# A hybrid decoder block: the recurrence's sigmoids written as tanh, side tasks cut into more steps, and a smaller permitted lag of side work

## The chip, the cores and the metric

One core of a Trainium2 chip runs the whole program. The metric is device time in microseconds (us), the median of several runs. Five engines work from queues of their own, each in the order in which the program gave it: PE (matrix products; PEld is its weight load), DVE (vector operations), ACT (functions by table, copies), POOL, and SP, which here only issues DMA transfers. An engine whose next instruction waits holds up everything queued behind it.

## What is computed

One decoder layer on x of 256 rows by 2048 columns, all in float32. RMS norm, then one input projection of 2048 to 15,904 columns, three token mixers (a gated linear recurrence; sparse attention over compressed, selected and window keys with 8 heads; forgetting attention with 8 heads), each multiplied by a SiLU gate, projected, scaled by a sigmoid merge gate and summed; an output projection; a gated per-layer embedding. The part that the change rewrites is the recurrence:

```python
rec = jax.nn.sigmoid(einsum(ub, wa) + ba)
inp = jax.nn.sigmoid(einsum(ub, wx) + bx)
log_a = -LRU_C * rec * jax.nn.softplus(-lam)     # LRU_C = 8
a = jnp.exp(log_a)
drive = jnp.sqrt(-jnp.expm1(2.0 * log_a)) * (inp * uc)
_, hseq = lax.associative_scan(linear_combine, (a, drive), axis=1)
```

## The kernel before

**The stream of weights.** All weights pass once through the core in 384 slices, most of 128 x 1024 numbers. I number them from 0 in the program's order; the code calls them `halves`. SP fetches a slice into one of five `raw` buffers. The slice is then cut into two parts, since products run in a rounded 32-bit type and the kernel wants more digits: ACT copies it to the rounded `wh`, then DVE forms the rest, `wl` = raw - wh (`cut`, `split`). PE multiplies wh by the high part of the left operand, wl by the high part, wh by its low part: 12 matmuls of 512 columns for a common slice. A slice of the compression (`cmp`; slices 38, 71 and 91 are such) takes only 8 matmuls of 256 columns, and costs ACT and DVE the same cut.

**The look-ahead.** wh and wl have four buffers (AHEAD + 1). The cut of slice i + 3 is written ahead of the matmuls of slice i, so cut i + 3 can begin when PE has done slice i - 1, and work that stands on ACT's queue behind cut i + 3 was placed there while slice i was being written.

**The side work.** Everything else is a set of generators: `lru_task` (recurrence, four of them, each for two column tiles), `nsa_task` (sparse attention, one for two heads and half of the rows), `fox_task`, `kk_task` and `norm_rows` (keys and queries normed and turned by DVE transposes and DMA, `cross`), `y_split` (gating and splitting a mixer's output for its projection), and so on. Twice per slice `Side.tick` runs a step of each active or urgent task, up to its next `yield`; what the step issues lands on the engines' queues between two cuts. `tick` stops when a clock kept while the program is written says that ACT or DVE would be more than LIMITS ns behind PE: one number for urgent tasks, one for the others, and another pair from the time the first queries (`q0`) are normed. `settle`, `powers` and `landed` let a task pause until that clock thinks that its engines or its DMA are through. So any edit of a task or limit re-deals the side work between the cuts. `need` would force tasks on if a slice's inputs weren't ready.

**The recurrence.** `lru_task` issues four gate functions for each of two column tiles (both results kept, from two PSUM banks, all eight in one step, then both banks given back), then per tile a Tanh of rec and an Exp of rec, a Square, a Sqrt, and DVE products and scans. ACT holds one table of functions at a time; a function of another table is preceded by an ACT_TABLE_LOAD. In a `soft` step of `nsa_task` DVE takes masked minima and ACT's three Exps follow in the same step.

**Names in profile rows.** All instructions have line L206, since one wrapper issues them; they are told by tile: `k_lru` (the recurrence's rec, inp, th), `k_uc`, `k_zt` (a chunk being turned), `k_th`/`k_gl`/`k_gn` (SiLU gates), `kk` (keys' split), `k_pz`/`sp_pc` (softmax), `k_mg` (merge gates), `k_yh`/`k_yl` (a mixer's output, split), `k_hnh`/`k_hnl` (normed input, split).

Of the kernel before, what the change touches and what calls it, by code (L numbers as in the profile page):

```python
# [12 lines left out]
AF = mybir.ActivationFunctionType  # L13
OP = mybir.AluOpType
# [28 lines left out]
VEC = {}  # L43
# [6 lines left out]
N_VEC = _at  # L50
# [273 lines left out]
def block_kernel(ctx: ExitStack, tc: tile.TileContext, io):  # L324
    nc = tc.nc
    clock = Clock()
    V, A, T, G, Q = (Metered(e, clock, n) for e, n in ((nc.vector, "v"), (nc.scalar, "a"), (nc.tensor, "pe"),
                                                      (nc.gpsimd, "g"), (nc.sync, "d")))
# [38 lines left out]
    side = Side(range(4), MOST, clock, ROOMS)  # L367
# [140 lines left out]
    def vcol(name, i=0):  # L508
        return vec[:, VEC[name] + i:VEC[name] + i + 1]
# [78 lines left out]
            split(hi[:, k, :], lo[:, k, :], x_tile(2 * i + k), x0[:, S + 2 * i + k:S + 2 * i + k + 1])  # L588

    def vec_task():  # L590
        a = VEC["lru_gate"]
        V.tensor_scalar(vec[:, a:], vec[:, a:], 0.5, None, op0=OP.mult)
        nl = sml([P, 8], name="nl")
        V.tensor_scalar(nl, vec[:, VEC["lam"]:VEC["lam"] + 8], -1.0, None, op0=OP.mult)
        yield from softplus(spc, nl, 8)
        V.tensor_scalar(spn, spc, -8.0, None, op0=OP.mult)
        V.tensor_scalar(spc, spc, 8.0, None, op0=OP.mult)

        V.scalar_tensor_tensor(gqn, vcol("nq"), SCALE, vcol("nk"), op0=OP.mult, op1=OP.mult)
        V.scalar_tensor_tensor(gqf, vcol("fq"), SCALE, vcol("fk"), op0=OP.mult, op1=OP.mult)  # L600
        yield True
# [58 lines left out]
    def cells(x):  # L660

        return x.rearrange("p (k i b) -> p b k i", b=4, i=32)
# [62 lines left out]
    def lru_task(i):  # L725
# [38 lines left out]
        for c in range(2):  # L764
            ct = 2 * i + c
            for s in range(2):
                g = banks[bs[c]][:, s * S:(s + 1) * S]
                A.activation(rec[own[s], c, :], g[own[s]], AF.Sigmoid, bias=vcol("ba", ct)[own[s]])
                A.activation(inp[own[s], c, :], g[other[s]], AF.Sigmoid, bias=vcol("bx", ct)[other[s]])
        side.back(*bs)  # L770
        yield True
        for c in range(2):
            ct = 2 * i + c
            A.activation(th[:, c, :], rec[:, c, :], AF.Tanh, scale=spc[:, ct:ct + 1])
        for c in range(2):
            ct = 2 * i + c
            A.activation(rec[:, c, :], rec[:, c, :], AF.Exp, scale=spn[:, ct:ct + 1])
        V.tensor_tensor(inp, inp, uc, op=OP.mult)
        yield True

        A.activation(uc, rec, AF.Square)
        V.scalar_tensor_tensor(th, uc, 1.0, th, op0=OP.add, op1=OP.mult)
        yield True
        A.activation(th, th, AF.Sqrt)
        V.tensor_tensor(th, th, inp, op=OP.mult)
        yield True
        for c in range(2):
# [109 lines left out]
    def nsa_task(g, pr, t):  # L897
# [19 lines left out]
        def soft(a, sc):  # L917

            for i, (o, x, msk) in enumerate(zip((pc[:, a, :], ps[:, a, 0, :], ps[:, a, 1, :]), sc,
                                                (cmask[:, t, :], mask[:, P * (2 - n):2 * P], mask[:, P:P + n * P]))):  # L920
                V.tensor_tensor_reduce(o, x, msk, -1.0, FLOOR, OP.add, OP.min, m[:, a, i:i + 1])
            for i, (o, x) in enumerate(((pc[:, a, :], pc[:, a, :]), (cell[:, a, 0], cells(ps[:, a, 0, :])),
                                        (cell[:, a, 1], cells(ps[:, a, 1, :])))):
                A.activation(o, x, AF.Exp, bias=m[:, a, i:i + 1], scale=-1.0, accum_out=s[:, a, i:i + 1])

        if t == 0:
            bs = yield from side.take(2)
            for a in range(2):
                mm3(banks[bs[a]][:, :272], qh[:, a, :], ql[:, a, :], kh[:, g, 128:400], kl[:, g, 128:400], True, True)
            yield True  # L930
            for a in range(2):
                x = banks[bs[a]]
                soft(a, (x[:, 128:144], x[:, 144:272], x[:, :128]))
                side.back(bs[a])
                yield True
        else:
            for a in range(2):
                b0, b1 = yield from side.take(2)
                mm3(banks[b0][:, :272], qh[:, a, :], ql[:, a, :], kh[:, g, :272], kl[:, g, :272], True, True)
                mm3(banks[b1][:, :256], qh[:, a, :], ql[:, a, :], kh[:, g, 272:], kl[:, g, 272:], True, True)  # L940
                yield True
                soft(a, (banks[b0][:, 256:272], banks[b1][:, :256], banks[b0][:, :256]))
                side.back(b0, b1)
                yield True
        side.give(k1=2)
# [4 lines left out]
        for a in range(2):  # L950
            V.tensor_scalar(pc3[:, a, :].rearrange("p (i c) -> p i c", i=3)[:, :, :16],
                            pc[:, a, None, :].to_broadcast([P, 3, 16]), s[:, a, 0:1], None, op0=OP.mult)
            for w in range(2):
                V.tensor_scalar(cell[:, a, w], cell[:, a, w], s[:, a, 1 + w:2 + w], None, op0=OP.mult)
        pt = pz.rearrange("p b n j -> p (b n j)")
        yield from cross(pt, pt, p)
        side.give(**{size: 1})
# [403 lines left out]
MARGIN = 1600.0  # L1361

LAND = 5500.0
LIMITS = ((3500.0, 2500.0), (4000.0, 3500.0))

CMP_FROM = 17

# [74 lines left out]
```

## Time and profile before

| | |
|---|---|
| median of 3 runs | 1074.49 us (1073.91 to 1074.62) |
| the profiled execution | 1074.18 us |
| its span, first to last instruction | 1072.4 us |
| PE busy | 1059.0 us, 99% |
| DVE, ACT busy | 771.2 us, 617.4 us |

The profile is of one execution. "Busy" counts a matmul from its start to its modelled end, and matmuls overlap: in a steady row a new one starts every 0.23 us and each counts 0.39 us. A short pause can therefore hide in the busy time; starts show it. An idle time in brackets is what the engine sat through before an instruction, with what ended it.

### The profile page before, as it was taken

How to read it: one execution, taken by the hardware profiler on the slowest of the kernel's cores; microseconds unless marked ns; L12 is line 12 of the kernel's file. 1: busy time of each engine (PE TensorE's matmuls, PEld its weight loads, DVE VectorE, ACT ScalarE, POOL GpSimd, SP SyncE). 2: the span in 40 equal slices, each digit the busy share in tenths (PEclk: the TensorE clock that was granted, in tenths of full speed). 3: DMA queues.
4: the chain of work that ended last, by engine and by line, in shares of the span. 5: the costliest groups of instructions: out<-in, count | busy, mean ns of one | idle time of the engine just before them, and what ended most of it. 6: DMA issues, size and time to landing. Idle time of an engine off the chain costs nothing.

```text
span 1072.4 us, 14101 instructions
## 1 busy us (share of the span) xinstructions
PE 1059.0 (99%) x4943; PEld 881.2 (82%) x4943; DVE 771.2 (72%) x1139; ACT 617.4 (58%) x917; POOL 51.1 (5%) x77
## 2 busy tenths in 40 slices
PE   9999999999999999999999999999999999999998
PEld 7887789887878878887888888888888888888886
DVE  7777699877787777778886866555776567666664
ACT  7668986776665565645645544465555444444442
POOL 0000000000000000001010000000000100000000
PEclk9999999999999999999999999999999999999999
DMA  9757768776666667558676776766676876788762
GB/s 340 251 186 220 255 219 266 243 240 193 214 206 195 198 200 221 159 172 281 201 224 210 226 217 184 236 216 204 206 255 199 264 248 212 228 253 262 264 215 79
DMA packets 86151, 237.54 MB, mean 222 GB/s; under 512 B 14008, under 2 KB 31040, under 8 KB 86080
## 3 DMA queue, kind: packets, MB, share of 16 engines
q1 hardware_dynamic: 81360, 220.89, 63.4%
q0 software_dynamic: 4720, 15.76, 5.7%
q8 instruction: 38, 0.62, 0.2%
q14 instruction: 33, 0.27, 0.1%
HBM read 215.62 MB, written 4.20 MB: 205 GB/s over the span
## 4 chain that ended last, share of the span: by engine, by line
PE 89%; ACT 4%; DVE 3%; DMA 2%; issue 2%; SPq 0%; DVEq 0%; ACTq 0%
PE main L206 85%; PE bank L206 4%; DVE wl L206 2%; ACT wh L206 2%; ACT k_lru L206 1%; DMA raw<-in_w 1%; DMA k_zn<-k_zt 1%; ACT L206 1%; SPq L206 0%; DVE k_zn L206 0%; ACT k_yh L206 0%; DVE k_fq L206 0%; DVE k_qn L206 0%; DVE k_zt L206 0%; DVE k_fin L206 0%
## 5 line engine op out<-in xcount | busy, mean ns | idle before, releaser
L206 DVE TENSOR_TENSOR wl<-raw,wh 128x1024 fp32r<-128x1024 f32 (+2 forms) x388 | 459.2, 1199 | 235.5 <-ACT wh L206 234.3
L206 ACT ACTIVATE wh<-raw 128x1024 fp32r<-128x1024 f32 (+2 forms) x388 | 397.9, 1039 | 291.3 <-PE main L206 258.4
L206 PE MATMUL main<-wh,k_hnh 128*128 128x512 f32 (+2 forms) x1026 | 395.8, 386 | 1.8 <-ACT wh L206 1.7
L206 PE MATMUL main<-wl,k_hnh 128*128 128x512 f32 (+2 forms) x1026 | 393.5, 384 | 3.4 <-DVE wl L206 3.3
L206 PE MATMUL main<-wh,k_hnl 128*128 128x512 f32 (+1 forms) x1024 | 392.7, 384 | 0.0
L206 PEld LDWEIGHTS main<-wl,k_hnh 128*128 128x128 f32 x1026 | 192.6, 188 | 41.6 <-DVE wl L206 6.5
L206 PEld LDWEIGHTS main<-wh,k_hnh 128*128 128x128 f32 x1026 | 193.0, 188 | 39.4 <-ACT wh L206 3.8
L206 PEld LDWEIGHTS main<-wh,k_hnl 128*128 128x128 f32 x1024 | 192.3, 188 | 37.7
L206 PE MATMUL main<-wl,k_yh 128*128 128x512 f32 x192 | 75.0, 391 | 1.0 <-DVE wl L206 1.0
L206 PE MATMUL main<-wh,k_yh 128*128 128x512 f32 x192 | 75.1, 391 | 0.5 <-ACT k_yh L206 0.5
L206 PE MATMUL main<-wh,k_yl 128*128 128x512 f32 x192 | 75.0, 390 | 0.0
L206 PE MATMUL main<-wh,k_mtl 128*128 128x512 f32 x128 | 49.9, 389 | 0.0
L206 PE MATMUL main<-wh,k_hth 128*128 128x512 f32 x128 | 49.8, 389 | 0.0
L206 PE MATMUL main<-wh,k_mth 128*128 128x512 f32 x128 | 49.8, 389 | 0.0
L206 PE MATMUL main<-wl,k_mth 128*128 128x512 f32 x128 | 49.8, 389 | 0.0
L206 PE MATMUL main<-wl,k_hth 128*128 128x512 f32 x128 | 49.8, 389 | 0.0
L206 PE MATMUL main<-wh,k_htl 128*128 128x512 f32 x128 | 49.8, 389 | 0.0
L206 PEld LDWEIGHTS main<-wl,k_yh 128*128 128x128 f32 x192 | 36.1, 188 | 9.0 <-DVE wl L206 1.7
L206 PEld LDWEIGHTS main<-wh,k_yh 128*128 128x128 f32 x192 | 36.1, 188 | 8.4 <-ACT k_yh L206 0.9
L206 PEld LDWEIGHTS main<-wh,k_yl 128*128 128x128 f32 x192 | 36.1, 188 | 7.9 <-DVE k_yl L206 0.4
L206 ACT ACTIVATE k_mg<-k_mg 128x512 f32<-128x512 f32 x24 | 15.2, 633 | 29.5 <-DVE k_mg L206 29.1
L206 PEld LDWEIGHTS main<-wh,k_htl 128*128 128x128 f32 x128 | 24.0, 188 | 5.0
(240 smaller groups left out, 957.0 us busy)
## 6 DMA issues: line engine op xcount, KB each, us to landing
raw<-in_w SPq DMA_DIRECT2D x369, 512.0 KB, 4.4
bias<-in_b_in POOLq DMA_DIRECT2D x21, 256.0 KB, 4.8
raw<-in_w SPq DMA_DIRECT2D x8, 408.0 KB, 3.8
k_pz<-k_prob SPq DMA_DIRECT2D x16, 128.0 KB, 3.9
e_dram<-k_e POOLq DMA_DIRECT2D x4, 512.0 KB, 3.7
k_merged<-k_zt SPq DMA_DIRECT2D x16, 128.0 KB, 2.9
k_xc<-in_x POOLq DMA_DIRECT2D x4, 512.0 KB, 5.2
k_hx<-k_zt SPq DMA_DIRECT2D x16, 128.0 KB, 3.0
```

The costliest lines, as they stand in the source:

```text
L206: r = call(out, *args, **kw)
```

## The change

Gates become `tanh(x/2)`, with the halving and the constant moved into scales, biases and vectors: sigmoid(x) = (1 + tanh(x/2))/2, so the Tanh and Exp of rec take the pointer `spc` or `spn` as bias too, the product with uc becomes a scalar_tensor_tensor, and Sqrt has a scale. The eight gate functions are in two steps, each giving back its bank. `soft` pauses between DVE's minima and ACT's Exps, and `nsa_task` once more ahead of its transposes. Beyond `q0` the permitted lag is 3000 and 2500 ns instead of 4000 and 3500.

```diff
@@ -588,13 +588,14 @@
             split(hi[:, k, :], lo[:, k, :], x_tile(2 * i + k), x0[:, S + 2 * i + k:S + 2 * i + k + 1])
 
     def vec_task():
-        a = VEC["lru_gate"]
-        V.tensor_scalar(vec[:, a:], vec[:, a:], 0.5, None, op0=OP.mult)
+
+        for cols in (slice(VEC["ba"], VEC["lam"]), slice(VEC["lru_gate"], N_VEC)):
+            V.tensor_scalar(vec[:, cols], vec[:, cols], 0.5, None, op0=OP.mult)
         nl = sml([P, 8], name="nl")
         V.tensor_scalar(nl, vec[:, VEC["lam"]:VEC["lam"] + 8], -1.0, None, op0=OP.mult)
         yield from softplus(spc, nl, 8)
-        V.tensor_scalar(spn, spc, -8.0, None, op0=OP.mult)
-        V.tensor_scalar(spc, spc, 8.0, None, op0=OP.mult)
+        V.tensor_scalar(spn, spc, -4.0, None, op0=OP.mult)
+        V.tensor_scalar(spc, spc, 4.0, None, op0=OP.mult)
 
         V.scalar_tensor_tensor(gqn, vcol("nq"), SCALE, vcol("nk"), op0=OP.mult, op1=OP.mult)
         V.scalar_tensor_tensor(gqf, vcol("fq"), SCALE, vcol("fk"), op0=OP.mult, op1=OP.mult)
@@ -765,23 +766,24 @@
             ct = 2 * i + c
             for s in range(2):
                 g = banks[bs[c]][:, s * S:(s + 1) * S]
-                A.activation(rec[own[s], c, :], g[own[s]], AF.Sigmoid, bias=vcol("ba", ct)[own[s]])
-                A.activation(inp[own[s], c, :], g[other[s]], AF.Sigmoid, bias=vcol("bx", ct)[other[s]])
-        side.back(*bs)
-        yield True
+                A.activation(rec[own[s], c, :], g[own[s]], AF.Tanh, bias=vcol("ba", ct)[own[s]], scale=0.5)
+                A.activation(inp[own[s], c, :], g[other[s]], AF.Tanh, bias=vcol("bx", ct)[other[s]], scale=0.5)
+            side.back(bs[c])
+            yield True
         for c in range(2):
             ct = 2 * i + c
-            A.activation(th[:, c, :], rec[:, c, :], AF.Tanh, scale=spc[:, ct:ct + 1])
+            A.activation(th[:, c, :], rec[:, c, :], AF.Tanh, scale=spc[:, ct:ct + 1], bias=spc[:, ct:ct + 1])
         for c in range(2):
             ct = 2 * i + c
-            A.activation(rec[:, c, :], rec[:, c, :], AF.Exp, scale=spn[:, ct:ct + 1])
-        V.tensor_tensor(inp, inp, uc, op=OP.mult)
+            A.activation(rec[:, c, :], rec[:, c, :], AF.Exp, scale=spn[:, ct:ct + 1], bias=spn[:, ct:ct + 1])
+        V.scalar_tensor_tensor(inp, inp, 1.0, uc, op0=OP.add, op1=OP.mult)
         yield True
 
         A.activation(uc, rec, AF.Square)
         V.scalar_tensor_tensor(th, uc, 1.0, th, op0=OP.add, op1=OP.mult)
         yield True
-        A.activation(th, th, AF.Sqrt)
+
+        A.activation(th, th, AF.Sqrt, scale=0.25)
         V.tensor_tensor(th, th, inp, op=OP.mult)
         yield True
         for c in range(2):
@@ -919,6 +921,7 @@
             for i, (o, x, msk) in enumerate(zip((pc[:, a, :], ps[:, a, 0, :], ps[:, a, 1, :]), sc,
                                                 (cmask[:, t, :], mask[:, P * (2 - n):2 * P], mask[:, P:P + n * P]))):
                 V.tensor_tensor_reduce(o, x, msk, -1.0, FLOOR, OP.add, OP.min, m[:, a, i:i + 1])
+            yield True
             for i, (o, x) in enumerate(((pc[:, a, :], pc[:, a, :]), (cell[:, a, 0], cells(ps[:, a, 0, :])),
                                         (cell[:, a, 1], cells(ps[:, a, 1, :])))):
                 A.activation(o, x, AF.Exp, bias=m[:, a, i:i + 1], scale=-1.0, accum_out=s[:, a, i:i + 1])
@@ -930,7 +933,7 @@
             yield True
             for a in range(2):
                 x = banks[bs[a]]
-                soft(a, (x[:, 128:144], x[:, 144:272], x[:, :128]))
+                yield from soft(a, (x[:, 128:144], x[:, 144:272], x[:, :128]))
                 side.back(bs[a])
                 yield True
         else:
@@ -939,7 +942,7 @@
                 mm3(banks[b0][:, :272], qh[:, a, :], ql[:, a, :], kh[:, g, :272], kl[:, g, :272], True, True)
                 mm3(banks[b1][:, :256], qh[:, a, :], ql[:, a, :], kh[:, g, 272:], kl[:, g, 272:], True, True)
                 yield True
-                soft(a, (banks[b0][:, 256:272], banks[b1][:, :256], banks[b0][:, :256]))
+                yield from soft(a, (banks[b0][:, 256:272], banks[b1][:, :256], banks[b0][:, :256]))
                 side.back(b0, b1)
                 yield True
         side.give(k1=2)
@@ -952,6 +955,7 @@
                             pc[:, a, None, :].to_broadcast([P, 3, 16]), s[:, a, 0:1], None, op0=OP.mult)
             for w in range(2):
                 V.tensor_scalar(cell[:, a, w], cell[:, a, w], s[:, a, 1 + w:2 + w], None, op0=OP.mult)
+        yield True
         pt = pz.rearrange("p b n j -> p (b n j)")
         yield from cross(pt, pt, p)
         side.give(**{size: 1})
@@ -1361,7 +1365,7 @@
 MARGIN = 1600.0
 
 LAND = 5500.0
-LIMITS = ((3500.0, 2500.0), (4000.0, 3500.0))
+LIMITS = ((3500.0, 2500.0), (3000.0, 2500.0))
 
 CMP_FROM = 17
```

ACT has 15 table loads before and 9 now. PE's matmuls are the same ones in number and kind; those of side tasks stand at other places. No slice's inputs are waited for by `need` in either program. From slice 224 on the cuts have the same side work between them (but for slices 275 and 276).

ACT at the first recurrence tasks (`wh_955` and `wh_956` are the cut of slice 36), before:

```order
L206 ACTIVATE wh_955<-raw_897 128x1024
L206 ACTIVATE k_zt_980<-main_83,rsr 128x16x32
L206 ACTIVATE k_zt_980<-main_84,rsr 128x16x32
L206 ACT_TABLE_LOAD
L206 ACTIVATE k_lru_984<-bank_87,vec 64x256
L206 ACTIVATE k_lru_985<-bank_87,vec 64x256
L206 ACTIVATE k_lru_984<-bank_87,vec 64x256
L206 ACTIVATE k_lru_985<-bank_87,vec 64x256
```

and now:

```order
L206 ACTIVATE wh_956<-raw_898 128x1024
L206 ACTIVATE k_zt_981<-main_83,rsr 128x16x32
L206 ACTIVATE k_zt_981<-main_84,rsr 128x16x32
L206 ACTIVATE k_lru_985<-bank_87,vec 64x256
L206 ACTIVATE k_lru_986<-bank_87,vec 64x256
L206 ACTIVATE k_lru_985<-bank_87,vec 64x256
L206 ACTIVATE k_lru_986<-bank_87,vec 64x256
L206 ACTIVATE wh_994<-raw_912 128x1024
L206 ACTIVATE wh_1008<-raw_936 128x1024
L206 ACTIVATE wh_1030<-raw_954 128x1024
```

The table load is gone, and four gate functions instead of eight stand ahead of the next three cuts.

ACT a little further, where two tasks meet (`wh_1047` is the cut of slice 40), before:

```order
L206 ACTIVATE wh_1047<-raw_995 128x1024
L206 ACTIVATE k_lru_986<-k_lru_984,spc 128x256 x2
L206 ACT_TABLE_LOAD
L206 ACTIVATE k_lru_984<-k_lru_984,spn 128x256 x2
L206 ACT_TABLE_LOAD
L206 ACTIVATE k_lru_1080<-bank_89,vec 64x256
L206 ACTIVATE k_lru_1081<-bank_89,vec 64x256
```

and now (`wh_1072` is the cut of slice 40):

```order
L206 ACTIVATE k_lru_1058<-bank_89,vec 64x256
L206 ACTIVATE k_lru_1059<-bank_89,vec 64x256
L206 ACTIVATE k_lru_987<-k_lru_985,spc 128x256 x2
L206 ACTIVATE k_lru_985<-k_lru_985,spn 128x256 x2
L206 ACTIVATE wh_1072<-raw_992 128x1024
L206 ACTIVATE wh_1090<-raw_1006 128x1024
L206 ACTIVATE wh_1104<-raw_1028 128x1024
```

Both table loads are gone here; the second task's first four gates stand ahead of the first task's Tanh and Exp, and this group stands ahead of cut 40 instead of behind it.

ACT at the keys' split (`wh_1756` is the cut of slice 70 in both), before:

```order
L206 ACTIVATE wh_1701<-raw_1616 128x544
L206 ACTIVATE wh_1717<-raw_1637 128x544
L206 ACTIVATE k_ucs_1419<-k_uc_1418 64x256 x2
L206 ACTIVATE wh_1756<-raw_1662 128x1024
L206 ACTIVATE kk<-k_zn_1507,gqn 128x128 x4
L206 ACTIVATE wh_1788<-raw_1699 128x1024
L206 ACTIVATE wh_1806<-raw_1715 128x1024
```

and now:

```order
L206 ACTIVATE wh_1704<-raw_1617 128x544
L206 ACTIVATE wh_1718<-raw_1638 128x544
L206 ACTIVATE k_ucs_1420<-k_uc_1419 64x256 x2
L206 ACTIVATE kk<-k_zn_1508,gqn 128x128 x4
L206 ACTIVATE wh_1756<-raw_1669 128x1024
L206 ACTIVATE kk<-k_zn_1508,gqn 128x128 x4
L206 ACTIVATE wh_1788<-raw_1702 128x1024
```

The first four `kk`, which need the transfer of `k_zn`, moved from behind cut 70 to ahead of it.

ACT at the last slices of the third merge chunk (`wh_3613` before and `wh_3660` now are the cut of slice 142), before:

```order
L206 ACTIVATE sp_pc_3542,sp_sm_3541<-sp_pc_3542,sp_m_3540 128x16
L206 ACTIVATE k_pz_3546,sp_sm_3541<-k_prob_3545,sp_m_3540 128x4x32 x2
L206 ACTIVATE wh_3589<-raw_3468 128x1024
L206 ACTIVATE sp_pc_3542,sp_sm_3541<-sp_pc_3542,sp_m_3540 128x16
L206 ACTIVATE k_pz_3546,sp_sm_3541<-k_prob_3545,sp_m_3540 128x4x32 x2
L206 ACTIVATE wh_3613<-raw_3498 128x1024
L206 ACTIVATE k_mg_3629<-k_mg_3629 128x512
L206 ACTIVATE k_mg_3630<-k_mg_3630 128x512
L206 ACTIVATE wh_3637<-raw_3547 128x1024
```

and now:

```order
L206 ACTIVATE wh_3615<-raw_3518 128x1024
L206 ACTIVATE wh_3634<-raw_3548 128x1024
L206 ACTIVATE sp_pc_3568,sp_sm_3567<-sp_pc_3568,sp_m_3566 128x16
L206 ACTIVATE k_pz_3572,sp_sm_3567<-k_prob_3571,sp_m_3566 128x4x2x32 x2
L206 ACTIVATE k_pct_3655<-bank_88 80x256
L206 ACTIVATE wh_3660<-raw_3588 128x1024
L206 ACTIVATE k_mg_3680<-k_mg_3680 128x512
L206 ACTIVATE k_mg_3681<-k_mg_3681 128x512
L206 ACTIVATE wh_3707<-raw_3613 128x1024
```

Of two pairs of Exps, each behind DVE's minima of its own step, one is left, and its minima stand two cuts earlier on DVE.

## Rows read from the trace of the kernel before

**Rows 1.** The page: the span and its instructions, and each engine's busy time, share of the span and instructions.

```profile
span 1072.4 us, 14101 instructions
...
PE 1059.0 (99%) x4943; PEld 881.2 (82%) x4943; DVE 771.2 (72%) x1139; ACT 617.4 (58%) x917; POOL 51.1 (5%) x77
```

**Rows 2.** The table by stretches of 20 us: length, busy time (and instructions) of PE, PEld, DVE, ACT and POOL, clock, DMA share, GB/s.

```profile
100.00:120.00 20.00, 17.23 (x80) 13.38 (x79) 8.29 (x8) 19.70 (x31) 0.00 (x0) 1.00 0.56 190
```

**Rows 3.** The chain that ended last, in order of time: start, length, what. The last long run of PE's weight matmuls, and a run of eight matmuls of a compression slice's size.

```profile
120.99 0.93 PE bank L206 x8
...
638.61 428.51 PE main L206 x1890
```

**Rows 4.** PE's instructions in order of time: start, length, what [idle before <- releaser]. Pairs of rows: the last matmul that started in step ahead of a pause, and the first that is in step behind it.

```profile
103.89 0.39 PE L206 MATMUL main<-wh,k_hnl 128*128 128x512 f32 x1
...
106.47 0.40 PE L206 MATMUL main<-wh,k_hnl 128*128 128x512 f32 x1
...
115.92 0.39 PE L206 MATMUL main<-wh,k_hnl 128*128 128x512 f32 x1
...
118.57 0.39 PE L206 MATMUL main<-wh,k_hnl 128*128 128x512 f32 x1
...
180.59 0.28 PE L206 MATMUL bank<-wh,k_xs 128*60 128x256 f32 x1
...
182.71 0.39 PE L206 MATMUL main<-wh,k_hnl 128*128 128x512 f32 x1
...
235.32 0.39 PE L206 MATMUL main<-wh,k_hnh 128*128 128x512 f32 x1
...
236.14 0.39 PE L206 MATMUL main<-wh,k_hnl 128*128 128x512 f32 x1
...
245.13 0.50 PE L206 MATMUL main<-wh,k_hnh 128*128 128x512 f32 x1
...
246.73 0.39 PE L206 MATMUL main<-wh,k_hnl 128*128 128x512 f32 x1
...
310.15 0.39 PE L206 MATMUL main<-wh,k_yl 128*128 128x512 f32 x1
...
312.11 0.40 PE L206 MATMUL main<-wh,k_yh 128*128 128x512 f32 x1
...
345.87 0.39 PE L206 MATMUL main<-wh,k_yh 128*128 128x512 f32 x1
...
346.79 0.40 PE L206 MATMUL main<-wh,k_yl 128*128 128x512 f32 x1
...
385.04 0.43 PE L206 MATMUL main<-wh,k_yh 128*128 128x512 f32 x1
...
386.57 0.40 PE L206 MATMUL main<-wh,k_yl 128*128 128x512 f32 x1
...
479.13 0.39 PE L206 MATMUL main<-wh,k_hnh 128*128 128x512 f32 x1
...
480.15 0.40 PE L206 MATMUL main<-wh,k_hnl 128*128 128x512 f32 x1
...
482.44 0.39 PE L206 MATMUL main<-wh,k_hnh 128*128 128x512 f32 x1
...
483.69 0.40 PE L206 MATMUL main<-wh,k_hnl 128*128 128x512 f32 x1
```

**Rows 5.** Who waited for whom, PE alone: us in total, times, longest us. `k_fx` are the forgetting attention's split operands.

```profile
PE bank L206 <- DVE k_fx L206: 0.5, 2, 0.2
```

**Rows 6.** ACT's instructions in order of time, at the first recurrence task: start, length, what [idle before <- releaser].

```profile
97.87 0.69 ACT L206 ACTIVATE k_zt<-main,rsr 128x512 f32<-128x512 f32 x1 [1.65 <-PE main L206]
98.58 1.28 ACT L206 ACT_TABLE_LOAD   x1
99.87 3.87 ACT L206 ACTIVATE k_lru<-bank,vec 64x256 f32<-64x256 f32 x8
103.76 3.90 ACT L206 ACTIVATE wh<-raw 128x1024 fp32r<-128x1024 f32 x4
107.57 0.89 ACT L206 ACTIVATE k_lru<-k_lru,spc 128x256 f32<-128x256 f32 x2
```

**Rows 7.** Groups of instructions by engine and operation: count | busy us, mean ns of one | idle before. `k_zt` has one pointer operand (the scale `rsr`), `k_e` has none; both read 512 columns of PSUM.

```profile
L206 ACT ACT_TABLE_LOAD x15 | 19.2, 1283 | 1.0 <-PEq L1435 0.7
L206 ACT ACTIVATE k_zt<-main,rsr 128x512 f32<-128x512 f32 x16 | 10.7, 684 | 6.7 <-PE main L206 6.7
L206 ACT ACTIVATE k_e<-main 128x512 f32<-128x512 f32 x8 | 4.8, 599 | 4.2 <-PE main L206 4.2
...
L206 DVE TENSOR_TENSOR wl<-raw,wh 128x1024 fp32r<-128x1024 f32 x369 | 444.2, 1219 | 233.0 <-ACT wh L206 231.9 <-DMA raw<-in_w 0.3
```

**Rows 8.** ACT in order of time at the third recurrence task, between the cuts of slices 85 and 86: start, length, what. Left out between the rows are a table load and eight gate functions.

```profile
207.17 1.14 ACT L206 ACTIVATE k_junk<-k_z 128x512 f32<-128x512 f32 x2
...
213.48 2.01 ACT L206 ACTIVATE wh<-raw 128x1024 fp32r<-128x1024 f32 x2
```

**Rows 9.** SP's and ACT's instructions in order of time at the keys' split.

```profile
167.98 2.56 SPq L206 DMA_DIRECT2D k_zn<-k_zt  x4
...
177.52 1.28 ACT L206 ACTIVATE kk<-k_zn,gqn 128x128 fp32r<-128x128 f32 x4 [3.62 <-DMA k_zn<-k_zt]
```

**Rows 10.** ACT in order of time at the third merge chunk: the merge gates and their wait.

```profile
382.68 1.29 ACT L206 ACTIVATE k_mg<-k_mg 128x512 f32<-128x512 f32 x2 [1.95 <-DVE k_mg L206]
```

## Prediction

> **What bounds the kernel now.** I read the page first: PE is busy for 1059.0 of 1072.4 us [rows 1]. The matmuls are the same ones after the change, so nearly all of the time is fixed, and what can be won lies in PE's pauses. The reader should not take the missing 13 us for them: busy time hides short pauses, and some of the 13 us are the start and the end, which the change doesn't touch. So I went to PE's starts. In its last long run 1890 weight matmuls take 428.51 us, 0.227 us each [rows 3]; whatever a start lies later than that is lost. From the last start in step to the first in step again, less 0.227 us for each step between (and 0.93 us for a compression slice's eight [rows 3]), the pauses are [rows 4]:
>
> - at 104 us 2.58 - 0.68 = 1.90, at 116 us 2.65 - 0.68 = 1.97; together 3.87 (A)
> - at 181 us 2.12 - 0.93 - 0.45 = 0.74 (B)
> - at 235 us 0.82 - 0.45 = 0.37, at 245 us 1.60 - 0.45 = 1.15; together 1.52 (C)
> - at 310 us 1.96 - 0.91 = 1.05 (D)
> - at 346 us 0.92 - 0.45 = 0.47 (E), at 385 us 1.53 - 0.45 = 1.08 (F)
> - at 479 us 1.02 - 0.45 = 0.57, at 482 us 1.25 - 0.45 = 0.80; together 1.37 (G)
>
> Sum 10.1 us, and two waits for the forgetting attention's operands with 0.5 us idle between them (H) [rows 5]. No change of side work alone can give much over 10.6 us. Then I asked what was late at each. In all but D and H it is a cut of weights, held up on ACT or DVE by side work. Between 100 and 120 us ACT is busy for 19.70 of 20 us and PE for 17.23, at the full clock of 1.00 [rows 2]: here ACT is the bound, for a short while. At E, F and G neither is full; they wait for each other in turn, and cuts stand behind the waiting instruction.
>
> **The gates.** ACT has six table loads fewer, 6 x 1.28 = 7.7 us [rows 7]. Sixteen Tanh and Exp instructions get a second pointer operand. No row has two; the nearest rows are one operand against none, 684 - 599 = 85 ns [rows 7]. The price lies between nothing and 0.17 us each; I take 0.085, 1.4 us in all. The 32 gates keep their size and the one pointer that they have, so I leave them at 0.48 us (3.87 for eight [rows 6]). The product that becomes a scalar_tensor_tensor and the extra small vector instruction are on DVE, under a tenth of a microsecond each and beside PE's work.
>
> A, worked out: before, a load and eight gates, 1.28 + 3.87 = 5.2 us, stand between cut 36 and cut 37, which so begins at 103.76 [rows 6]. Now four gates stand there: from the end of k_zt at 98.56, 1.92 us later cut 37 begins, at 100.5, 3.3 us sooner. That pause goes. The second moves: ahead of cut 40 now stand eight gates, two Tanhs and two Exps, 3.87 + 0.89 + 0.91 + 4 x 0.085 = 6.0 us. By sums: 98.56 + 1.92 + three cuts of 0.97 (3.90 / 4 [rows 6]) + 6.0 = 109.4; the cut takes about 1.0 and wl 1.22 us [rows 7], which gives 111.6. PE, unpaused, would begin slice 37 at 104.12 + 0.93, since the second task's gate products now stand in slice 36; then 37, 38 and 39 at 2.72 + 0.93 + 2.72 us end at 111.42, and wl is wanted 0.23 later, at 111.65. It just fits. A like block did fit before: 6.3 us, from 207.17 to 213.48 [rows 8], without a pause behind it. I leave 0.1 us: **A gives 3.8**, between 2.9 (a late start of a microsecond) and 3.87.
>
> C: before, load and eight gates and Square again stood in one block. Now the largest block there is four gates, load and Sqrt, 1.92 + 1.28 + 0.5 = 3.7 us, then two cuts, then load, Tanhs and Exps, 1.28 + 1.80 + 0.34 = 3.4 us. Neither reaches the 6.3 us that fitted [rows 8], but they lie close. I leave 0.2: **C gives 1.3**, between 0.5 and 1.5.
>
> What a switch of tables costs: ACT's load at 98.58 follows the end of k_zt at 98.56 and the first gate starts at 99.87, right behind its 1.28 us [rows 6]: the switch costs 1.3 us and nothing more is seen. The Trainium skill (ScalarE: Activation LUTs, "What ACT_TABLE_LOAD costs") adds a drain of about 1380 ns to a load of about 1283 ns, 2.66 us for each switch. By that rule ACT would save 16 us instead of 7.7, and the two loads left in C's stretch would cost more than I count. The load's length agrees with the trace, the drain does not show, and the measurement decides here.
>
> **The shorter steps and limits.** E and F are the ping-pong: ACT sat 1.95 us ahead of the merge gates, with three cuts behind it [rows 10]. Before, two pairs of minima and Exps stood right ahead of it in adjoining cuts; now one, whose minima stand two cuts earlier, so its Exps find them done. What is late next is the merge gates themselves, which wait for PE's own last matmul of the chunk and for one DVE pass. **E and F give 1.5**, between 0.5 and 1.55. G: the splits for the second projection and the turning of the queries, with DVE and ACT alternating, stood within three cuts; they now stand at cuts 167 to 169 and 174, apart, since the attention tasks end sooner. **G gives 1.4**, between 0.5 and 1.4. The limits issue nothing; through them the rest moves.
>
> **What stays.** D: the last split ahead of the first projection stands at cut 120 in both programs, behind the same merge gates: 0. H: the cuts and splits there are the same: 0.
>
> **What it costs.** B: four `kk` stand ahead of cut 70 now, and they wait for the transfer of k_zn; behind them are cut 70, cut 71 and all of ACT. Before, the transfer went out at 167.98 and was awaited until 177.52 [rows 9]. Now it is one weight fetch earlier on SP's queue, at about 166.8. If it lands as long after its issue, kk starts at 176.4, and 1.2 (kk) + 1.0 + 1.2 give wl 70 at 179.8, where PE wants it at 178.1 (180.59 [rows 4] less 2.72, plus 0.23): a pause of 1.7 us. If it lands 2 us sooner, none. With 0.74 there already, **B** is between +0.7 and -1.0; I take 0. At slice 103 four groups of attention products now stand half a slice to a slice and a half behind the split that feeds them, where before it was two slices: one bounded wait, between 0 and 1.5, I take 0.5. Elsewhere the side work of slices 84 to 222 is dealt anew; a pause of the kind of E could arise anywhere there, and I take one, 0.5, between 0 and 2.
>
> **Sum.** 3.8 + 1.3 + 1.5 + 1.4 - 0.5 - 0.5 = 7.0 us. The profiled execution took 1074.18 us, 1.78 beyond its span; 1067.2 now. The median of the runs is 0.31 above that execution: **1067.5 us**. The terms' bounds give 10 to 3 us of gain; mixed, 1065 to 1070 is this case's own range.
>
> **Rivals.**
>
> 1. *The pauses move and don't close* (0.22). ACT and DVE still have to do the work ahead of its readers, and only 6.3 us of ACT's 617 go. If cut 40 is a microsecond late, kk costs its 1.7 instead of 0.74, and the attention products and one more chain 1.5 each, 3.5 us come back: 1071. For it: the sums at cut 40 fit with nothing to spare. Against: no block now is larger than one that fitted.
> 2. *No effect* (0.08), 1074.5: the loads were beside the point, and what held the cuts were weight transfers. Against it: PE's pauses end on wh and wl while ACT is full.
> 3. *Slower* (0.05): k_zn's transfer now stops ACT ahead of cut 70, and each microsecond that it lands after 174.7 is one that PE loses. It has to be 8 us late to eat the rest, landing near 183; then about 1077. The 9.5 us from issue to kk in [rows 9] speak against it.
> 4. *A switch stops ACT for about twice its load* (0.05), 1.28 us more than the load's own time. Then the two loads between cuts 91 and 94 push these 2.6 us further, which uses up C's gain and 0.7 more: 1067.5 + 2.0 = 1069.5. The contiguous rows at 98.56 to 99.87 [rows 6] speak against it. The rule of the Trainium skill named above would do this.
>
> **How the numbers follow.** The forecast has 0.60. What a measurement here can tell from no change is about 0.2%, 2.1 us. The forecast, rival 4 and nearly all of rival 1 are faster by more: 0.85. Rival 2 and a little of 1: same, 0.10. Slower: 0.05. The range goes from 1064, where B, C and E end at their best and nothing new arises, to 1072, which takes in most of rival 1; it leaves out some 0.17.
>
> **What would show it.** ACT with 9 loads; between 100 and 120 us PE busy for the full 20; no pause over 0.3 us at cuts 37 and 40; the gates at about 0.47 us; a kk wait ahead of cut 70, with a pause up to 1.7 us; no pause near 346, 385 and 480 us; D and H as before. A pause over 1 us at cut 40, or new pauses between 200 and 470 us of more than 2 us together, would prove the sum wrong.

## The result and the profile after

The changed kernel takes 1066.87 us (median of 4 runs, 1066.32 to 1067.2) against 1074.2 us before (4 runs): a ratio of 0.9932, 95% interval 0.9916 to 0.9947. It is 0.7% faster. The profiled execution took 1066.59 us. Its page, span and busy times, which answer to [rows 1], with the engines' shares of the chain of waits:

```profile
span 1064.8 us, 14107 instructions
...
PE 1055.4 (99%) x4943; PEld 881.1 (83%) x4943; DVE 771.3 (72%) x1140; ACT 611.4 (57%) x911; POOL 54.2 (5%) x77
...
PE 94%; DVE 2%; DMA 1%; ACT 1%; issue 1%; SPq 0%; DVEq 0%; ACTq 0%
```

The same number of matmuls, 7.6 us less span, 6.0 us less work on ACT. Groups of ACT's instructions (count | busy us, mean ns of one | idle before), which answer to [rows 6, 7]:

```profile
L206 ACT ACTIVATE k_lru<-bank,vec 64x256 f32<-64x256 f32 x32 | 14.9, 467 | 0.4
L206 ACT ACT_TABLE_LOAD x9 | 11.5, 1283 | 0.9 <-PEq L1439 0.7
L206 ACT ACTIVATE k_lru<-k_lru,spc 128x256 f32<-128x256 f32 x8 | 4.4, 592 | 0.0
L206 ACT ACTIVATE k_lru<-k_lru,spn 128x256 f32<-128x256 f32 x8 | 4.3, 590 | 0.0
```

Nine loads; a gate costs 0.47 us as before. The table by stretches, between 100 and 120 us (columns as in [rows 2]), and ACT in order of time there (as in [rows 6]):

```profile
100.00:120.00 20.00, 20.00 (x102) 16.83 (x101) 12.98 (x16) 19.80 (x34) 0.00 (x0) 1.00 0.75 264
```

```profile
98.17 0.69 ACT L206 ACTIVATE k_zt<-main,rsr 128x512 f32<-128x512 f32 x1 [1.65 <-PE main L206]
98.75 1.92 ACT L206 ACTIVATE k_lru<-bank,vec 64x256 f32<-64x256 f32 x4
100.70 2.96 ACT L206 ACTIVATE wh<-raw 128x1024 fp32r<-128x1024 f32 x3
103.56 3.87 ACT L206 ACTIVATE k_lru<-bank,vec 64x256 f32<-64x256 f32 x8
107.45 1.09 ACT L206 ACTIVATE k_lru<-k_lru,spc 128x256 f32<-128x256 f32 x2
108.45 1.08 ACT L206 ACTIVATE k_lru<-k_lru,spn 128x256 f32<-128x256 f32 x2
109.44 2.94 ACT L206 ACTIVATE wh<-raw 128x1024 fp32r<-128x1024 f32 x3
```

ACT is as full as it was, 19.80 of 20 us, and yet PE no longer waits. Cut 37 starts at 100.70 instead of 103.76 and cut 40 at 109.44, where the prediction had 109.4.

Three things are left in the middle of the program: B, D and H. PE's starts at B and at D (start, length, what [idle before <- releaser]):

```profile
177.81 0.28 PE L206 MATMUL bank<-wl,k_xs 128*60 128x256 f32 x1
178.20 0.50 PE L206 MATMUL main<-wh,k_hnh 128*128 128x512 f32 x1
179.46 0.50 PE L206 MATMUL main<-wl,k_hnh 128*128 128x512 f32 x1 [0.76 <-DVE wl L206]
...
307.05 0.39 PE L206 MATMUL main<-wh,k_yl 128*128 128x512 f32 x1
307.69 0.50 PE L206 MATMUL main<-wh,k_yh 128*128 128x512 f32 x1 [0.26 <-ACT k_yh L206]
```

D is 0.80 us (1.05 before). B is 1.42 (0.7 before). What holds it are not the keys' operands but the weights of cuts 70 and 72, as ACT in order of time shows:

```profile
168.74 1.28 ACT L206 ACTIVATE kk<-k_zn,gqn 128x128 fp32r<-128x128 f32 x4
171.69 1.06 ACT L206 ACTIVATE wh<-raw 128x1024 fp32r<-128x1024 f32 x1 [1.67 <-DMA raw<-in_w]
172.66 1.27 ACT L206 ACTIVATE kk<-k_zn,gqn 128x128 fp32r<-128x128 f32 x4
173.83 1.04 ACT L206 ACTIVATE wh<-raw 128x1024 fp32r<-128x1024 f32 x1
177.09 1.06 ACT L206 ACTIVATE wh<-raw 128x1024 fp32r<-128x1024 f32 x1 [2.21 <-DMA raw<-in_w]
```

The first kk starts with no wait at 168.74, where [rows 9] had 3.62 us; cut 72, for which PE stops, waits 2.21 us for its raw.

**The pauses of every kernel.** The letters are the prediction's places; the kernels are described further down. For each profiled execution I summed what PE's starts lose against the usual distance of their group, leaving out losses under 0.22 us, as in the prediction's list (the two ways of counting differ by under 0.1 us a pause). The last column is the profiled time less the sum.

| kernel | A | B | C | D | E, F | G | H | others | sum | time less sum |
|---|---|---|---|---|---|---|---|---|---|---|
| before | 3.88 | 0.67 | 1.51 | 1.05 | 1.54 | 1.36 | 0.68 | 0 | 10.7 | 1063.5 |
| changed | 0 | 1.42 | 0 | 0.80 | 0 | 0 | 0.67 | 0 | 2.9 | 1063.7 |
| old order, fewer loads | 0.49 | 1.98 | 0 | 1.00 | 1.59 | 1.36 | 0.68 | 0 | 7.1 | 1064.8 |
| new order, old loads | 2.71 | 0 | 2.40 | 0.79 | 0 | 0 | 1.35 | 0 | 7.3 | 1063.5 |
| tanh alone | 0.48 | 2.64 | 0.40 | 0 | 1.07 | 1.36 | 0.68 | 0.51 | 7.1 | 1063.2 |
| steps and limits alone | 0.58 | 0.27 | 0 | 5.16 | 0 | 0 | 0.68 | 0.53 | 7.2 | 1063.9 |
| gates in one step | 0.49 | 1.99 | 0 | 3.50 | 0 | 0 | 0.68 | 0.49 | 7.2 | 1063.8 |
| old limits | 0 | 1.55 | 0 | 5.43 | 0 | 0 | 0.68 | 0.53 | 8.2 | 1063.0 |
| attention steps undone | 0 | 0.22 | 0 | 7.10 | 0 | 0 | 0.72 | 1.37 | 9.4 | 1063.4 |
| k_zn on POOL's queue | 0 | 0.25 | 0 | 0.80 | 0 | 0 | 1.80 | 0 | 2.9 | 1063.4 |
| no tanh, early splits | 0.59 | 0.32 | 2.41 | 0 | 0 | 0 | 3.82 | 0.77 | 7.9 | 1063.5 |
| steps undone, early splits | 0 | 0.91 | 0 | 0 | 0 | 4.45 | 0.34 | 1.90 | 7.6 | 1062.6 |
| early splits | 0 | 0 | 0 | 0 | 0 | 0 | 0.68 | 0.57 | 1.3 | 1063.6 |
| both repairs | 0 | 0 | 0 | 0 | 0 | 0 | 0.68 | 0.57 | 1.3 | 1063.4 |

The last column lies between 1062.6 and 1063.9, but for one kernel (1064.8, whose first products waited some 1.5 us more at the start). So nearly all of what tells these kernels apart is in the pauses. Of the 11 executions of the kernel with gates in one step, one took 2974.59 us and is left out of its ratio.

### The profile page after: what moved, and what is told of

Same layout as the page of the kernel before. It is cut to its first block, busy times and chain, and to the rows that moved or that the text cites. A ratio compares the mean times of both kernels' runs of the same rounds, so it can differ in the third digit from the quotient of the medians.

```text
span 1064.8 us, 14107 instructions
## 1 busy us (share of the span) xinstructions
PE 1055.4 (99%) x4943; PEld 881.1 (83%) x4943; DVE 771.3 (72%) x1140; ACT 611.4 (57%) x911; POOL 54.2 (5%) x77
## 4 chain that ended last, share of the span: by engine, by line
PE 94%; DVE 2%; DMA 1%; ACT 1%; issue 1%; SPq 0%; DVEq 0%; ACTq 0%
PE main L206 89%; PE bank L206 5%; DMA raw<-in_w 1%; ACT wh L206 1%; DVE wl L206 1%; DVE k_zn L206 0%; DVE k_yl L206 0%; SPq L206 0%; DVE k_fin L206 0%; DVE k_mg L206 0%; DVE k_fx L206 0%; DVE k_uc L206 0%; ACT L206 0%; DVE k_z L206 0%; DVE sp_nss L206 0%
## 5 line engine op out<-in xcount | busy, mean ns | idle before, releaser
L206 PEld LDWEIGHTS main<-wh,k_mth 128*128 128x128 f32 x128 | 24.0, 188 | 5.0
```

The lines of the kernel that those rows point to most:

```text
L206: r = call(out, *args, **kw)
```

## Experiments

**Loads against order.** Two kernels keep every instruction of a program in its place on every engine and change only the function that the gates execute (the order is planned with the one function, `real` is the one that ACT gets), so that only the table loads differ. Old order, fewer loads:

```diff
-A.activation(rec[...], g[...], AF.Sigmoid, bias=...)      # inp alike
+A.activation(rec[...], g[...], AF.Sigmoid, bias=..., real=AF.Exp)
```

> The kernel before with every instruction in its old place on every engine; only the gates are executed as Exp instead of Sigmoid, so the outputs of the recurrence are others and ACT has 7 table loads instead of 15. Theory (the loads hold the cuts at A and C): the load ahead of the first gates goes, so the pause at 104 us falls from 1.90 to about 0.6; two more loads go ahead of cut 40, which is more than its pause of 1.97; C's 1.52 goes too. Sum 3.3 + 1.5 = 4.8: 1069.4 us, with E, F and G still there (2.9 us). Rival (only the order of the side work counts, the loads are beside the point): 1074 us, A and C as before. Second rival (a load costs ACT twice its length): A and C are gone as well, but ACT's rows shorten by 2.6 us a load, not by 1.3.

Measured: 1070.31 us (ratio 0.996, 0.9949 to 0.9972). A falls to 0.49, C to nothing, E, F and G stay, as the theory had it. B grows by 1.3 us, so part of the gain is given back. PE comes there 2.2 us sooner, the first kk only 0.7: from the first issue of the transfer of k_zn, at 166.00, to kk it is 10.8 us, where [rows 9] had 9.5. Cut 71 stands behind the four kk:

```profile
176.84 1.28 ACT L207 ACTIVATE kk<-k_zn,gqn 128x128 fp32r<-128x128 f32 x4 [4.90 <-DMA k_zn<-k_zt]
178.06 1.06 ACT L207 ACTIVATE wh<-raw 128x1024 fp32r<-128x1024 f32 x1
```

ACT at the first recurrence task:

```profile
99.29 0.69 ACT L207 ACTIVATE k_zt<-main,rsr 128x512 f32<-128x512 f32 x1 [1.65 <-PE main L207]
99.88 3.86 ACT L207 ACTIVATE k_lru<-bank,vec 64x256 f32<-64x256 f32 x8
103.76 3.91 ACT L207 ACTIVATE wh<-raw 128x1024 fp32r<-128x1024 f32 x4
```

The gates start 0.59 us after the last k_zt, before it ends; with the load ahead of them it was 2.00 us [rows 6]. The difference of 1.41 us is what the pause at 104 us fell by, from 1.90 to 0.49.

The reverse, new order, old loads:

```diff
-A.activation(rec[...], g[...], AF.Tanh, bias=..., scale=0.5)      # inp alike
+A.activation(rec[...], g[...], AF.Tanh, bias=..., scale=0.5, real=AF.Sigmoid)
```

> The changed kernel with every instruction in its place; only the gates are executed as Sigmoid of x/2 instead of Tanh, so the outputs of the recurrence are others and ACT has 16 table loads instead of 9. Theory (the loads hold the cuts at A and C): four loads come back ahead of cut 40, 5.1 us, against a spare of 0.28 us there: A about 4.8 us again; at C three come back against a spare of 0.6: 1 to 3 us. Sum 1066.9 + 4.8 + 2 = 1073.7, between 1071.5 and 1075; E, F and G stay closed. Rival (only the order counts): 1067 us.

Measured: 1073.16 us (0.9988, 0.9979 to 0.9997); the profiled execution 1070.74. A and C are back with 2.71 and 2.40 us, E to G stay closed. At A I had counted four loads ahead of cut 40; the trace has two:

```profile
98.98 1.28 ACT L207 ACT_TABLE_LOAD   x1
100.27 1.92 ACT L207 ACTIVATE k_lru<-bank,vec 64x256 f32<-64x256 f32 x4
102.22 2.96 ACT L207 ACTIVATE wh<-raw 128x1024 fp32r<-128x1024 f32 x3
105.08 3.85 ACT L207 ACTIVATE k_lru<-bank,vec 64x256 f32<-64x256 f32 x8
108.96 1.10 ACT L207 ACTIVATE k_lru<-k_lru,spc 128x256 f32<-128x256 f32 x2
110.07 1.28 ACT L207 ACT_TABLE_LOAD   x1
111.37 1.09 ACT L207 ACTIVATE k_lru<-k_lru,spn 128x256 f32<-128x256 f32 x2
112.37 1.04 ACT L207 ACTIVATE wh<-raw 128x1024 fp32r<-128x1024 f32 x1
```

Each load takes 1.28 us and the next instruction starts 1.29 to 1.30 after its start. The whole price is a little higher, since without a load an ACTIVATE starts about 0.1 us before the one ahead of it ends, and the load takes that overlap away: at the 15 loads in which the kernels of these two pairs differ (8 and 7), the two instructions around it start 1.39 to 1.42 us further apart with it than without. Two loads, 2.8 us, less the spare of 0.28 are 2.5 us; the rest of the 2.71 is what PE loses as it starts again. Both kernels show the loads to hold the cuts at A and C, and the rival of order alone falls there.

**Each half alone.** The tanh alone (gates in one step, old limits, no new pauses in the attention):

> The kernel before with the sigmoids written as tanh, and nothing else: gates in one step, old limits, no pause in the attention's steps. Theory (tanh closes A and C, the steps and limits close E, F and G): 1074.2 - 3.9 - 1.3 = 1069 us, with 2.9 us left at E, F and G; if the eight gates in one step are too long a block ahead of a cut, some of A stays, up to 1 us. Rival (tanh alone moves the pauses about): 1071 to 1074.

Measured: 1072.04 us (0.9971, 0.9961 to 0.9981), profiled 1070.31. A is 0.48, C 0.40, F and G stay. But B is 2.64 (kk waits 4.45 us for k_zn, and cuts 71 and 72 stand behind it) and a wait of 0.51 is new, and D and E have closed without anything in the edit that aims at them. The divided steps and limits alone, with the sigmoids as they were:

> The changed kernel with the sigmoids as they were before: divided steps and new limits alone. Theory: E, F and G are closed (2.9 us), A and C still hold the cuts, since five table loads stand there again; the divided gates make A's blocks shorter, which may take a microsecond of A. 1074.2 - 2.9 = 1071.3, down to 1070. Rival (re-dealing does it all): 1067.

Measured: 1070.62 us (0.9963, 0.9951 to 0.9974). E and G closed and only 0.53 us left near F, as expected. A is 0.58 and C 0 with the loads still there: the divided gates and another order do for these cuts nearly what the missing loads do. So fewer loads suffice for A and C, but they aren't the only way. D took 5.16 us. That the time is where the theory had it is luck: A and C lost 4.8 us less than before, D 4.1 us more.

**One part of the change undone.** The eight gates in one step again:

```diff
-            side.back(bs[c])
-            yield True
+        side.back(*bs)
+        yield True
```

> The changed kernel with one part undone: the eight gates of a task stand in one step again and give back both banks together. Theory (at A the length of the block ahead of a cut decides): eight gates, 3.87 us, instead of 1.92 ahead of cut 37, so a pause near 105 us comes back, 0.4 to 0.6 us; the rest as in the changed kernel: 1067.4. Rival (the division opens both A pauses): 1070, with over 2 us at A.

Measured: 1072.48 us (0.9986, 0.9977 to 0.9996), profiled 1070.92. A is 0.49 as the theory said, but B and D cost 1.99 (kk waits 3.35 us for k_zn) and 3.50. The old limits:

```diff
-LIMITS = ((3500.0, 2500.0), (3000.0, 2500.0))
+LIMITS = ((3500.0, 2500.0), (4000.0, 3500.0))
```

> The changed kernel with the old limits of 4000 and 3500 ns. Theory (the divided attention steps close E, F and G, the limits only help): at most one of the three comes back, 0 to 1 us: 1067 to 1068. Rival (the limits close them): all three come back, 2.9 us: 1069.8. A and C closed in both.

Measured: 1071.21 us (0.9968, 0.9957 to 0.9978). E, F and G are closed without the lower limits, though 0.53 is new at 403 us; D costs 5.43. The two new pauses in the attention task undone:

```diff
                 V.tensor_tensor_reduce(o, x, msk, -1.0, FLOOR, OP.add, OP.min, m[:, a, i:i + 1])
-            yield True
...
-        yield True
         pt = pz.rearrange("p b n j -> p (b n j)")
```

> The changed kernel without the two new pauses in the attention task (minima and Exps in one step again, no pause ahead of the transposes). Theory (the divided steps close E, F and G): they come back, up to 2.9 us: 1068.5 to 1069.8. Rival (the limits do it): 1067, no pause over 0.3 us between 330 and 490 us.

Measured: 1072.82 us (0.9985, 0.9976 to 0.9994). E, F and G are closed at their places without these either. But at the merge gates after F's, near 424 us, there is a new pause of 1.37 us, and it is of E's kind: ACT sits ahead of the merge gates, two cuts stand behind them, and PE waits for the wl of one.

```profile
422.56 1.29 ACT L206 ACTIVATE k_mg<-k_mg 128x512 f32<-128x512 f32 x2 [4.47 <-DVE k_mg L206]
423.76 1.99 ACT L206 ACTIVATE wh<-raw 128x1024 fp32r<-128x1024 f32 x2
...
426.11 0.50 PE L206 MATMUL main<-wl,k_yh 128*128 128x512 f32 x1 [0.76 <-DVE wl L206]
```

So this run doesn't acquit the undivided steps; the pause may only have moved. D costs 7.10. ACT, PE's first start behind the pause and the table by stretches there:

```profile
301.16 1.29 ACT L206 ACTIVATE k_mg<-k_mg 128x512 f32<-128x512 f32 x2 [1.95 <-DVE k_mg L206]
302.36 1.99 ACT L206 ACTIVATE wh<-raw 128x1024 fp32r<-128x1024 f32 x2
306.42 0.63 ACT L206 ACTIVATE k_yh<-k_yl 128x512 fp32r<-128x512 f32 x1 [2.08 <-DVE k_yl L206]
306.96 1.04 ACT L206 ACTIVATE wh<-raw 128x1024 fp32r<-128x1024 f32 x1
309.89 0.63 ACT L206 ACTIVATE k_yh<-k_yl 128x512 fp32r<-128x512 f32 x1 [1.89 <-DVE k_yl L206]
...
307.10 0.79 PE L206 MATMUL main<-wh,k_yh 128*128 128x512 f32 x1 [4.07 <-ACT k_yh L206]
```

```profile
304.00:306.00 2.00, 0.00 (x0) 0.00 (x0) 2.00 (x3) 0.34 (x1) 0.00 (x0) 1.00 0.74 191
306.00:308.00 2.00, 0.90 (x2) 0.67 (x3) 1.08 (x2) 1.58 (x2) 0.00 (x0) 0.60 0.70 221
308.00:310.00 2.00, 2.00 (x6) 1.60 (x6) 1.83 (x2) 0.11 (x1) 0.00 (x0) 0.50 0.99 205
310.00:312.00 2.00, 2.00 (x7) 1.52 (x6) 1.27 (x5) 0.52 (x1) 0.00 (x0) 0.50 0.78 293
```

Of the four splits for the first projection, two stand behind the merge gates here: one behind two cuts, the last behind a third cut as well. PE stops for 4.1 us; as it goes on, the granted clock falls from 1.00 to 0.50 (0.60 is the mean of both in the row from 306 us), and matmuls of 512 columns start 0.43 us apart instead of 0.23. In the changed kernel one split stands behind the merge gates, two cuts behind them, which costs 0.80; with the old limits it is three cuts, which costs 5.43; two splits cost 3.50 to 7.10; none, 0.

**Is D the cause of these losses, and can it be taken away?** The four splits are started four slices sooner and ahead of other urgent tasks, and each waits for its own recurrence task only (`early splits`):

```diff
-                q[0]["starts"] = (f"ysplit{b}",)
+                (out[-4] if b == 0 else q[0])["starts"] = (f"ysplit{b}",)
...
+            if not heads:
+                yield from side.wait(f"lru{i // 2}")
...
-            side.urge(name, y_split(name, st["yl"], [f"lru{q}" for q in range(4)] + ["gl0", "gl1"], st["gl"], False))
+            side.urgent.insert(0, (name, y_split(name, st["yl"], ["gl0", "gl1"], st["gl"], False)))
```

Steps and limits without tanh, with early splits (the last two recurrence tasks made urgent as well, or they end too late):

> The divided steps and limits with the sigmoids as they were, as in the run of steps and limits alone, but with the four splits for the first projection ahead of its merge gates: they are started four slices sooner, each waits for its own recurrence task only, and the last two recurrence tasks are urgent. Theory (that run lost 5.2 us at D alone, and the loads themselves matter only at A, 0.6 us): D is gone, 1070.6 - 5.2 + up to 1 for the new places of the recurrence = 1065.5 to 1066.5, no slower than the changed kernel. Rival (the loads cost where they stand, and cost more when the tasks run closer together): pauses of 2 us or more between 100 and 290 us, 1068 to 1070.

Measured: 1069.39 us (0.9949, 0.9936 to 0.9963). D is gone, but 2.41 us are back at C, and the profiled execution has 3.82 at H. Place and time are the rival's. The attention steps undone, with early splits:

> The changed kernel without the two new pauses in the attention task, and with the four splits for the first projection early (started four slices sooner, each waiting for its own recurrence task only). Theory (the run without these pauses lost 7.1 us at D alone, and E, F and G are closed by the lower limits as well): D is gone, 1072.8 - 7.1 = 1065.7, up to 1067 with the 1.4 us at 424 us. Rival (the divided steps themselves are worth something): E, F or G open again, 1068 to 1070.

Measured: 1070.24 us (0.9958, 0.9945 to 0.997). D is gone and 2.6 us come of it, not 7.1: G has 4.45 us now, and 1.90 lie between 412 and 462 us, 0.69 of them again at merge gates ahead of which ACT sat 4.32 us. The rival, that the divided steps are worth something, is nearer.

Put together by the table, the stretch behind D up to H (318 to 494 us: E, F, G and what of "others" lies there) loses 1.4 to 6.4 us in the five kernels without the new pauses in the attention task (before, old order with fewer loads, tanh alone, and the two with these steps undone) and at most 0.6 in the nine that have them, with old limits (0.53) as with new ones. That speaks for the divided steps and not for the limits. It isn't shown: every one of these edits re-deals the side work, and no run takes the pauses out with the order held fixed.

The changed kernel with early splits:

> The changed kernel with one repair: the four splits for the first projection early, as above. Theory: D's 0.8 us goes and nothing else changes: 1066.9 - 0.8 = 1066.1, granted clock at 1.0 throughout. Rival (the dealing of the side work behind it opens another pause): 1067 and more.

Measured: 1065.75 us (0.9917, 0.9903 to 0.9931). D is gone; 0.57 us are new at 471.

**B.** The turning of the keys on POOL's queue:

```diff
-            Q.dma_start(to[:, a, :], ...)
+            queue.dma_start(to[:, a, :], ...)     # queue is G for the keys, Q for all others
```

> The changed kernel with one edit: the four transfers that turn the keys (k_zn) go out on POOL's queue instead of SP's, where they took 2.5 us between two weight fetches. Theory for B (the weight fetches of slices 70 to 72 go out late on SP, and cut 72 waits for its raw): the fetch of slice 70 goes out near 164 instead of 165.8, cuts 70 and 72 wait less, B falls from 1.42 to 0.3 or less: 1065.6. Rival 1 (the DMA engines are full there, in whatever order): B stays at 1.2 or more: 1066.9. Rival 2 (kk's wait decides after all): POOL's queue brings k_zn later, kk waits, and B grows over 2 us: 1067.5 and more.

Measured: 1065.71 us (0.9919, 0.9905 to 0.9932), B 0.25. This looks like the theory, but it settles nothing: the kernel with early splits has SP's old order at B and has no pause there. (H is 1.80 in the profiled execution, so the sum of its pauses, 2.9, is that of the changed kernel.) In the kernel with early splits ACT has, in order of time:

```profile
172.27 1.06 ACT L206 ACTIVATE wh<-raw 128x1024 fp32r<-128x1024 f32 x1 [2.04 <-DMA raw<-in_w]
173.24 1.26 ACT L206 ACTIVATE kk<-k_zn,gqn 128x128 fp32r<-128x128 f32 x4
174.41 1.04 ACT L206 ACTIVATE wh<-raw 128x1024 fp32r<-128x1024 f32 x1
176.09 1.06 ACT L206 ACTIVATE wh<-raw 128x1024 fp32r<-128x1024 f32 x1 [0.64 <-DMA raw<-in_w]
```

Cut 72 starts at 176.09 here and at 177.09 in the changed kernel; what PE loses turns on this one transfer. With the same instructions up to there, B was 1.42, 1.55, 0.22, 0.91 and 0 in five executions. In none of the five does kk wait, so that rival falls for this order; what sets the landing of the raw stays open. The DMA engines' busy share from 172 to 178 us is 1.0 with the pause (0.99 to 1.04 in the changed kernel) and without it (1.00 to 1.03 with early splits), so that they are full doesn't tell the two apart. In the five kernels whose first four kk stand behind cut 70 (before, old order with fewer loads, tanh alone, steps and limits alone, gates in one step) they do wait, 1.19 to 4.90 us, and B is 0.27 to 2.64: there the transfers of k_zn landed 4.8 to 6.0 us after their issue (medians). In the six that have kk ahead of cut 70 and the transfers on SP's queue it is 2.7 to 2.9 us.

Both repairs:

> The changed kernel with both repairs: the splits early, and the four transfers that turn the keys on POOL's queue. Theory (B and D are independent): 1066.9 - 0.8 - 1.1 = 1065.0. Rival (the time won at B and D is given back where a transfer is late, as at 496 us in the run with POOL's queue, 1.46 us instead of 0.34): 1065.7 or more.

Measured: 1065.52 us (0.9914, 0.99 to 0.9928). The best, with a gain over the changed kernel of 1.3 us between medians; the intervals against the kernel before overlap, and the two repairs don't add up (1065.71, 1065.75 and 1065.52).

## Why the prediction was right, point by point

- **A, 3.8 forecast, 3.88 measured; C, 1.3 and 1.5.** The mechanism is shown: with the order held fixed, taking loads away closes A to 0.49 and C to nothing, and putting them back opens both. Cut 40 fitted, as the sum had it, and with more to spare: its wl was done 0.28 us before PE wanted it, where the prediction had 0.05. What it said of a switch, "1.3 us and nothing more is seen", is 0.1 us short: 1.39 to 1.42 us from start to start. It counted in the rows of one kernel, and the overlap that is lost shows only beside a kernel without the load.
- **E and F, 1.5 and 1.54; G, 1.4 and 1.36.** The sizes held, the reason isn't shown. I put them down to the divided minima and Exps and to the splits standing apart; yet these places are closed too in three kernels that lack the lower limits, the divided attention steps or the tanh. Over the whole stretch the kernels bear out the divided steps (1.4 to 6.4 us lost without them, at most 0.6 with them; G opened to 4.45 in a kernel without them), but which place closes depends on how the side work happens to be dealt.
- **D, forecast unchanged, 0.25 better.** Right, since the order shows the split at the same cut. But I gave it no bound. It was the dearest place of the redealing: one cut further, or one split more, and the change would have lost 3.5 to 7.1 us, as four of the kernels did. Rival 1 had the right mechanism and half the price.
- **B, forecast 0, measured 0.7 worse.** The step that failed: "they wait for the transfer of k_zn". The transfers landed 2.7 us after their issue (median; 2.7 to 2.9 in all six kernels with this order, 4.8 to 6.0 in the five with the old one), kk started 5.5 us after the first issue where the prediction had taken over 9.5, and it didn't wait; cut 72's weights were late. That the bound of 0.7 held was luck: another mechanism reached it, one which varies between executions of the same instructions by 1.5 us.
- **The two halves of a microsecond** for slice 103 and for a pause dealt anew did not come; they pay for B. In all the pauses shrank by 7.8 us (10.7 to 2.9), where the sum had 7.0, and the time beside them grew by 0.2. In kernels with other deals such pauses are there, 0.5 to 1.9 us.
- **Prices on ACT.** A load 1.28, a gate 0.47, a second pointer 592 ns against 496 with one in the kernel of the old order: 0.096 us, where I took 0.085.

```profile
L207 ACT ACTIVATE k_lru<-k_lru,spc 128x256 f32<-128x256 f32 x8 | 3.6, 496 | 0.8 <-DVE sp_nss L207 0.8
```

The Trainium skill (ScalarE: Activation LUTs, "What ACT_TABLE_LOAD costs") gives about 93 ns for each pointer operand; the trace agrees. Its drain of about 1380 ns at a load is in neither kernel: the gates follow the start of the load at 98.98 by 1.29 us, and the whole switch costs 1.39 to 1.42. By that rule rival 4 would have come true.

## What to carry to other kernels

Where an engine is full for a short stretch, price the block that stands ahead of the next needed operand, not the engine's total: in the old order eight loads fewer, 10.3 us of ACT's time, gave 4.9 us, and only at two places; 1.3 of it went again at B. When an edit re-deals side work, look up in the new order where the operand with the nearest reader now stands and price the case that it slips by one place; that price, not the edit's, may be the larger one. And before a gain is put down to one part of a change, undo the others too: here each part undone took away about half of the gain or more, mostly at places that it doesn't touch.

## What the runs showed of the hardware

- A switch of ACT's table costs more than its load: the load takes 1.28 us, and the instructions around it start 1.39 to 1.42 us further apart than without it (15 loads, two pairs of kernels with the same order), since the overlap of about 0.1 us between neighbours goes too.
- After PE's longest pauses the granted clock fell to 0.50 (1.2 of 2.4 GHz) for some microseconds: after an idle time of 4.1 us (attention steps undone) a loss of 2.87 us more, after 3.4 (old limits) and 3.2 us (steps and limits alone) of 1.84 each. After an idle time of 2.24 us at D (gates in one step), and in the kernel before after losses of 1.97, it stayed at 1.00. It is not the length of one pause alone: it also fell to 0.50 at 484 us after idle times of 1.6 and 0.8 us (attention steps undone, early splits) and at 502 us after 0.6 and 0.9 us (steps and limits without tanh, early splits).
- Three kernels (new order with old loads, tanh alone, gates in one step) have medians 1.6 to 2.4 us over their profiled executions. Their executions of 1071.9 to 1075.3 us have a mean granted clock of 0.996 to 0.998, the shorter ones, with those that were profiled, 0.999 or 1.0. Which pauses are behind this no trace shows.
